# Two token groups for expert 0, more expert weights loaded ahead, and a dispatch that turns tokens by block transposes

## The chip, the cores and the metric

The kernel runs on one core of a Trainium2 chip. The metric is the device time of one execution in microseconds, the median of several. Engines are named as in the profile: PE is TensorE, PEld its loads of weights, DVE is VectorE, ACT is ScalarE, POOL is GpSimd and SP is SyncE, from which the weights' transfers are issued.

## The reference, cut to what matters

Two layers of an encoder on 256 tokens of width 1024. Each layer mixes (convolution and attention), then feeds forward: the first layer with a dense SwiGLU, the second with eight experts of which each token takes two. The change is in this last part:

```python
def moe_swiglu(h, w_router, b_router, w_gate, w_up, w_down):
    t = h.reshape(B * S, D)                                   # 256 x 1024
    logits = (t @ w_router).astype(jnp.float32) + b_router.astype(jnp.float32)
    top_val, top_idx = lax.top_k(logits, TOP_K)               # 2 of 8
    top_w = jax.nn.softmax(top_val, axis=-1)
    combine = jnp.sum(jax.nn.one_hot(top_idx, N_EXPERTS, dtype=jnp.float32)
                      * top_w[..., None], axis=1).astype(t.dtype)
    out = jnp.zeros_like(t)
    for e in range(N_EXPERTS):
        out = out + combine[:, e:e + 1] * swiglu(t, w_gate[e], w_up[e], w_down[e])
    return out.reshape(B, S, D)
```

Each expert has weights of 1024 x 3584 for gate, the same for up, and 3584 x 1024 for down, in float32: 42 MiB an expert, 336 MiB in all. Here `t` is the modulated, normalised residual `x`. With the reference's inputs expert 0 gets 34 tokens and the others 99, 66, 75, 39, 78, 58 and 63.

## The kernel before, in words

**Trunk.** The first layer and the mixing of the second come first and take some 520 us. The expert part follows.

**Slots.** The experts are worked on in eight slots. Slot 0 is always expert 0; slots 1 to 7 are the other experts, sorted by their number of tokens, which the kernel finds out as it runs. A slot has room for `CAPS[e]` groups of 32 tokens. A slot with four groups (slot 1) is *wide*: its matmuls run in three passes on weights split in two parts, hi (`half_hi`, on ACT, L147) and lo (`half_lo`, on DVE, L155), of 1 MiB of weights each. All other slots are *narrow*: the tokens are the stationary operand, 32 columns at a time, four column groups of the array work side by side, and the weights move as they were loaded (`streams`, L1096). If a slot's room isn't enough, a loop behind the kernel (`rest`) redoes the expert part for what was left over; it is not entered with these inputs.

**Units.** A slot's work is cut into seven units. One unit is gu, the gate and up products for 512 hidden columns (4 MiB of weights), and dn, the down product for them (2 MiB). In the program the dn of a unit stands behind the gu of the unit after it. Two lanes of slots (`LANES`) run by turns, lane 1 beginning after three units of lane 0 (`STAGGER`). Between gu and dn of a narrow unit stand silu and product (`sg`, `mh`), and `h_T`, which turns the hidden values by 16 block transposes on DVE (hT, L1141). Where a wide unit follows, these transposes are put off into the middle of it.

**Dispatch.** Ahead of a slot's first unit, `dispatch` brings its tokens into the slot's order: `slot_pick` makes a selection matrix `pm`; `gather` multiplies `x_sb` (the tokens, as stationary operand) with `pm` as moving operand, two halves of 16 matmuls (L1036), so that the result has the model's width on the partitions; ACT scales and shifts it by the modulation (xf, L1040); DVE copies it into the slot's `xn` (L1060). Behind it come small matmuls (`ps_ws`) for the gates and `pmT`, from which `combine` later returns the results to the tokens' order. The dispatch of a lane's next slot stands behind gu of the last but one unit of the slot before, so that it falls between two units of the other lane.

**Loads.** The weights come in half chunks of 1 MiB, all issued from SP in the order of use, each into a buffer of some pool (`raw`, `hi`, `lo`, or the working tiles `a8` of 1 MiB and `a4` of half a MiB). A load waits for whoever used its buffer last. `need(k)` issues all loads up to chunk k; `mk` in it chooses the pool by the half chunk's number `m`. `EARLY` says how many chunks are asked for before the expert part's schedule begins; the first 16 half chunks, by `SPARE8` and `SPARE4`, can lie in tiles that the trunk uses elsewhere.

**Order.** In the expert part the program's order is the engines' order (`tc.manual_schedule`); each engine works in order and waits where an operand isn't ready.

Of the kernel before, what the change touches and what calls it, by code (L numbers as in the profile page):

```python
# [9 lines left out]
F32 = mybir.dt.float32  # L10
# [20 lines left out]
PT1 = (29, 49, 15, 36)  # L31
RAW = 9
AUX = 29
SPARE8 = (0, 10, 11)
SPARE4 = (1, 6, 8)
EARLY = 7
CAPS = (3, 4, 3, 3, 3, 2, 2, 2)
LANES = (0, 1, 2, 3), (5, 6, 4, 7)
STAGGER = 3
HOME = (0, None, 0, None, 768, 768, 1536, 1536)  # L40
NR = NE - 1
EPS = 1e-6
NORM = D ** 0.5 / -8192.0
# [11 lines left out]
def kernel(ctx, tc, x, cvec, wada, bada, wga, wqkv, wout, wfgu, wfd, wfd2,  # L55
# [12 lines left out]
    def bank(name):  # L68
        return pb.tile([P, 512], F32, tag="b", name=name)
# [59 lines left out]
    def load(ap, n=4096, mk=lambda s: (rawp, "raw", G)):  # L129

        raw = []
        for h in range(n // G):
            src = ap[h] if isinstance(ap, list) else ap[:, h * G:h * G + G]
            pool, tag, w = mk(h)
            raw.append([])
            for o_ in range(0, G, w):
                r = pool.tile([P, w], F32, tag=tag, name="raw", bufs=bufs.get(tag))
                nc.sync.dma_start(r, src[:, o_:o_ + w])
                raw[-1].append(r)
        return raw  # L140
# [61 lines left out]
    def need(k):  # L202
        while len(raws) <= min(k, len(plan) - 1):
            i = len(raws)
            ap, n = plan[i]

            def mk(h):
                m = 2 * (i - first_gu) + h
                if m in SPARE8:
                    return pools["wk"], "a8", G  # L210
                if m in SPARE4:
                    return pools["wk"], "a4", G // 2
                if i < first_gu + 6:
                    return rawp, "raw", G
                turn[0] += 1
                if any(n_ for _, n_ in plan[i - 6:i + 3]):
                    return (rawp, "raw", G) if turn[0] % 10 else (pools["wk"], "a8", G)
                at = turn[0] % 16
                return ((rawp, "raw", G), (hip, "hi", G), (lop, "lo", G), (pools["wk"], "a8", G))[
                    (at >= 9) + (at >= 12) + (at >= 15)]  # L220

            raws.append(load(ap() if callable(ap) else ap, n or 4096, mk))

    def ahead(nhi, nlo=None, pre=True):
# [20 lines left out]
    def whole(lead=1):  # L245

        k = [i for i, (_, n) in enumerate(plan) if n == 0][wholes[0]]
        wholes[0] += 1
        need(k + lead)

        def rows(h, i):

            r = raws[k][h]
            n = 4 // len(r)
            return r[i // n][:, i % n * 512:i % n * 512 + 512]
        return rows
# [661 lines left out]
    def moe(acc, g_bc, mm, A, B, AW, bw):  # L918
# [109 lines left out]
        def gather(pm, n, put):  # L1028

            for q in range(2):  # L1030
                ps = bank("ps_g").rearrange("p (j s) -> p j s", j=4)
                f = a2("xf", [P, 4, P])
                for j in range(4):
                    k = 4 * q + j
                    for t in range(NT):
                        nc.tensor.matmul(ps[:, j, 0:n], x_sb[:, t, k * P:(k + 1) * P], pm[:, 1, t, 0:n],  # L1036
                                         start=t == 0, stop=t == NT - 1)
                for j in range(4):
                    k = 4 * q + j
                    nc.scalar.activation(f[:, j, 0:n], ps[:, j, 0:n], AF.Identity, scale=A[:, k:k + 1],  # L1040
                                         bias=B[:, k:k + 1])
                put(slice(4 * q, 4 * q + 4), f[:, :, 0:n])

        def dispatch(e, pm):


# [12 lines left out]
                def put(js, f):  # L1059
                    nc.vector.tensor_copy(xg[:, js, :], f)  # L1060

            gather(pm, n, put)
            ps = bank("ps_ws")
            ws = sm.tile([P, 4], F32, tag="ws", name="ws")

# [470 lines left out]
```

## Time and profile before

| | |
|---|---|
| median of 3 runs | 1374.87 us (1374.77 to 1375.17) |
| the profiled execution, its own time | 1380.11 us |
| its span, first to last instruction | 1378.4 us |
| mean granted clock of PE | 0.988 |
| PE busy | 1316.5 us (96%) |
| DVE busy | 773.1 us (56%) |
| ACT busy | 371.4 us (27%) |
| moved by DMA | 473.64 MB, mean 344 GB/s |

All times in views are microseconds from the start of the span. The profiled execution is 5.2 us longer than the median of the timed ones; what is worked out from its rows has to be set against its own time. Busy shares are over the whole span, and the expert part (from 523.7 us) has stages with different limits, so they are read by stage. PE counts as busy from the start of a matmul to its modelled end, and matmuls of the four column groups overlap, so that a PE shown as busy can still wait for little things.

### The profile page before, as it was taken

The numbers are of one execution on the slowest core, as the hardware profiler recorded it, in microseconds if no ns is written. First come the engines' busy times: TensorE is split into PE (matmuls) and PEld (weight loads), VectorE is DVE, ScalarE is ACT, GpSimd is POOL, SyncE is SP. The second block draws the span as 40 slices with busy tenths as digits, with TensorE's granted clock in tenths as the row PEclk, the third lists the DMA queues.
The fourth block names the chain that finished last, engine by engine and source line by source line (L and its number), as shares of the span: only waits on it lengthen the run. The fifth ranks groups of instructions, "written<-read, shape, count | busy, mean of one in ns | idle before, by whom it ended". The sixth has DMA issues, their size and how long they took to land.

```text
span 1378.4 us, 38871 instructions
## 1 busy us (share of the span) xinstructions
PE 1316.5 (96%) x17220; PEld 971.7 (70%) x17220; DVE 773.1 (56%) x1832; ACT 371.4 (27%) x574; POOL 3.1 (0%) x18
## 2 busy tenths in 40 slices
PE   4998989999989899999999999999999999999996
PEld 4877689999788676666667667766766776666663
DVE  3498677777679955234476666753343343334253
ACT  3335344444364522101244345401000000100000
POOL 0000000000000000000000000000000000000000
PEclk9999999999999999999999999999999999999998
DMA  9972687888561549999989999999999999999994
GB/s 384 400 291 82 256 298 282 305 300 299 196 235 41 183 154 372 402 420 425 363 354 427 398 419 407 399 411 425 423 425 423 425 424 424 400 420 417 424 425 188
DMA packets 66383, 473.64 MB, mean 344 GB/s; under 512 B 7840, under 2 KB 7968, under 8 KB 9248
## 3 DMA queue, kind: packets, MB, share of 16 engines
q1 hardware_dynamic: 66208, 471.09, 84.7%
q8 instruction: 137, 2.24, 0.6%
q14 instruction: 38, 0.31, 0.1%
HBM read 470.01 MB, written 1.05 MB: 342 GB/s over the span
## 4 chain that ended last, share of the span: by engine, by line
PE 81%; DMA 8%; DVE 6%; ACT 3%; issue 1%; SPq 0%; ACTq 0%; DVEq 0%
PE ps_gu L1096 26%; PE ps_d L1096 13%; DMA raw<-in_wmd 4%; PE ps_ga L267 4%; PE ps_ga L265 4%; PE ps_ga L266 4%; DMA raw<-in_wmgu 3%; PE ps_g L1036 2%; PE ps_y L719 2%; PE ps_gu L267 2%; PE ps_gu L265 2%; PE ps_gu L266 2%; DVE cv L555 2%; PE ps_ada L319 2%; DVE lo L155 1%; PE ps_f L265 1%
## 5 line engine op out<-in xcount | busy, mean ns | idle before, releaser
L1096 PE MATMUL ps_gu<-raw,xn 128*32 128x256 f32 x8064 | 445.8, 379 | 1.3 <-DMA raw<-in_wmgu 0.7
L1096 PEld LDWEIGHTS ps_gu<-raw,xn 128*32 128x32 f32 x8064 | 279.7, 110 | 155.9 <-issue 2.4
L155 DVE TENSOR_TENSOR lo<-raw,hi 128x2048 fp32r<-128x2048 f32 x99 | 225.8, 2290 | 79.5 <-ACT hi L147 79.0
L1096 PE MATMUL ps_d<-raw,hT 128*32 128x256 f32 x4032 | 228.4, 379 | 2.6 <-DMA raw<-in_wmd 2.4
L1130 DVE TENSOR_TENSOR mh<-ps_gu,sg 128x256 f32<-128x256 f32 (+1 forms) x91 | 32.5, 382 | 343.0 <-ACT sg L1127 342.8
L147 ACT ACTIVATE hi<-raw 128x2048 fp32r<-128x2048 f32 x99 | 188.3, 1913 | 113.2 <-PE ps_ga L267 43.0
L1141 DVE STREAM_TRANSPOSE hT<-mh 32x96 f32<-32x96 f32 (+1 forms) x784 | 200.2, 255 | 13.5 <-PE ps_bc L384 0.2
L1096 PEld LDWEIGHTS ps_d<-raw,hT 128*32 128x32 f32 x4032 | 136.2, 110 | 85.1 <-DMA raw<-in_wmd 4.0
L1127 ACT ACTIVATE sg<-ps_gu 128x256 f32<-128x256 f32 (+1 forms) x91 | 31.9, 351 | 567.1 <-PE ps_gu L1096 521.8
L265 PE MATMUL ps_ga<-hThi,lo 128*128 128x256 f32 x480 | 137.9, 287 | 7.5 <-ACT hThi L457 7.5
L267 PE MATMUL ps_ga<-hTlo,hi 128*128 128x256 f32 x480 | 137.1, 286 | 0.5 <-DVE hTlo L462 0.5
L266 PE MATMUL ps_ga<-hThi,hi 128*128 128x256 f32 x480 | 136.6, 285 | 0.0
L265 PEld LDWEIGHTS ps_ga<-hThi,lo 128*128 128x128 f32 x480 | 93.2, 194 | 8.6 <-ACT hThi L457 8.4
L267 PEld LDWEIGHTS ps_ga<-hTlo,hi 128*128 128x128 f32 x480 | 92.5, 193 | 1.2 <-DVE hTlo L462 1.2
L266 PEld LDWEIGHTS ps_ga<-hThi,hi 128*128 128x128 f32 x480 | 92.8, 193 | 0.2
L555 DVE SCALAR_TENSOR_TENSOR cv<-zp,cols_sb,cv 128x256 f32<-128x256 f32 x206 | 85.4, 476 | 0.0
L358 DVE SCALAR_TENSOR_TENSOR ada_acc<-raw,cs,ada_acc 128x512 f32<-128x512 f32 x63 | 47.2, 749 | 1.2
L267 PE MATMUL ps_gu<-lo,xg 128*128 128x512 f32 x112 | 44.5, 397 | 1.6 <-DVE lo L155 1.6
L265 PE MATMUL ps_gu<-hi,xg 128*128 128x512 f32 x112 | 44.5, 397 | 0.0
L266 PE MATMUL ps_gu<-hi,xg 128*128 128x512 f32 x112 | 44.1, 394 | 0.0
L319 PE MATMUL ps_ada<-raw,crep 128*32 128x128 f32 x960 | 34.3, 302 | 7.6 <-DMA raw<-in_wada 7.2
L319 PEld LDWEIGHTS ps_ada<-raw,crep 128*32 128x32 f32 x960 | 29.1, 121 | 11.4 <-issue 8.6
(265 smaller groups left out, 1269.1 us busy)
## 6 DMA issues: line engine op xcount, KB each, us to landing
raw<-in_wmgu SPq DMA_DIRECT2D x222, 1024.0 KB, 15.0
raw<-in_wmd SPq DMA_DIRECT2D x111, 1024.0 KB, 15.7
raw<-in_wada SPq DMA_DIRECT2D x48, 1024.0 KB, 6.3
raw<-in_wfgu SPq DMA_DIRECT2D x22, 1024.0 KB, 5.9
raw<-in_wqkv SPq DMA_DIRECT2D x12, 1024.0 KB, 6.9
raw<-in_wfd SPq DMA_DIRECT2D x11, 1024.0 KB, 6.8
raw<-in_wga SPq DMA_DIRECT2D x8, 1024.0 KB, 11.1
raw<-in_wout SPq DMA_DIRECT2D x8, 1024.0 KB, 7.0
```

Source lines behind the costliest of these rows:

```text
L147: nc.scalar.activation(hi[:, i * w:(i + 1) * w], r, AF.Copy)
L155: nc.vector.tensor_tensor(lo[:, w], r, hi[:, w].bitcast(F32), op=ALU.subtract)
L265: nc.tensor.matmul(o_, a[1], b[0], start=first, stop=False)
L266: nc.tensor.matmul(o_, a[0], b[0], start=False, stop=False)
L267: nc.tensor.matmul(o_, a[0], b[1], start=False, stop=last)
L319: nc.tensor.matmul(ps[32 * g:32 * g + 32, 0:P], crep[:, j, :], w(j)[:, g * P:(g + 1) * P], start=j == 0, stop=j == KT - 1)
L358: nc.vector.scalar_tensor_tensor(accs[ch], ws[ch](j), cs[:, j:j + 1], accs[ch], op0=ALU.mult, op1=ALU.add)
L555: nc.vector.scalar_tensor_tensor(cv[:, a, :], zp[:, a, i:i + S], cw[:, a, i:i + 1], cv[:, a, :], op0=ALU.mult, op1=ALU.add)
L1096: nc.tensor.matmul(ps[t // 2][32 * j:32 * j + 32, t % 2], x(t), w(j), start=first and t % 2 == 0, stop=last, skip_group_check=True)
L1127: nc.scalar.activation(sg[:, 2 * b:2 * b + m, :], v[:, 0:m, 0, :], AF.Silu)
L1130: nc.vector.tensor_tensor(hm[:, 2 * b:2 * b + m, :], v[:, 0:m, 1, :], sg[:, 2 * b:2 * b + m, :], op=ALU.mult)
L1141: nc.vector.transpose(hT[32 * q:32 * q + 32, :, j], v[32 * j:32 * j + 32, :, q])
```

## The change

Four things change. (1) `CAPS[0]` goes from three groups to two, and lane 1 runs slots 4, 5, 6, 7 where it ran 5, 6, 4, 7; `HOME` (where a slot's `xn` lies) follows. (2) Instead of 16 half chunks, 20 have a buffer of their own ahead of the expert part: the string `FIRST` names a pool for each ("8" and "4" are `a8` and `a4`, r, h, l are `raw`, `hi`, `lo`), `RING` for those behind where no wide unit is near, and `EARLY` is 9. (3) The last chunk, the down weights of the last unit, is loaded in eight pieces of 256 KB, by rows in the order of use. (4) Narrow slots other than slot 0 are dispatched by `spread` in place of `gather`: `pm` is the stationary operand, 32 columns of it, and `x_sb` moves, 256 columns at a time, in four column groups. The result has the tokens on the partitions; for each half ACT copies it to SBUF (`tk`), 16 block transposes on DVE turn it (xf), and ACT scales and shifts it into `xn`.

```diff
-SPARE8 = (0, 10, 11)
-SPARE4 = (1, 6, 8)
-EARLY = 7
-CAPS = (3, 4, 3, 3, 3, 2, 2, 2)
-LANES = (0, 1, 2, 3), (5, 6, 4, 7)
+FIRST = "84rrrr4rhlrhlhl488rr"
+RING = "rrrrrhlrhlhlr8rr"
+EARLY = 9
+CAPS = (2, 4, 3, 3, 3, 2, 2, 2)
+LANES = (0, 1, 2, 3), (4, 5, 6, 7)
...
             def mk(h):
                 m = 2 * (i - first_gu) + h
-                if m in SPARE8:
-                    return pools["wk"], "a8", G
-                if m in SPARE4:
-                    return pools["wk"], "a4", G // 2
...
+                if m < len(FIRST):
+                    at = FIRST[m]
...
+            if i == len(plan) - 1:
+
+                raws.append([])
+                for j, src in enumerate(zip(*[v.rearrange("p (k n) -> k p n", k=4) for v in ap()])):
+                    r = rawp.tile([P, 2, 512], F32, tag="raw", name="raw")
+                    for h in range(2):
+                        nc.sync.dma_start(r[:, h, :], src[h])
+                    raws[-1].append(r)
+                continue
...
+        def spread(pm, g, xg):
+
+
+            pv = [bank(f"ps_g{b}").rearrange("p (t s) -> p t s", t=2) for b in range((g + 1) // 2)]
+            for t in range(g):
+                for tt in range(NT):
+                    for j in range(4):
+                        nc.tensor.matmul(pv[t // 2][32 * j:32 * j + 32, t % 2], pm[:, 1, tt, 32 * t:32 * t + 32],
+                                         x_sb[:, tt, 256 * j:256 * j + 256], start=tt == 0 and t % 2 == 0,
+                                         stop=tt == NT - 1, skip_group_check=True)
+            for h in range(2):
+                tk = a2("tk", [P, g, P])
+                for b, v in enumerate(pv):
+                    m = min(2, g - 2 * b)
+                    nc.scalar.activation(tk[:, 2 * b:2 * b + m, :], v[:, 0:m, h * P:h * P + P], AF.Copy)
+                v = tk.rearrange("p t (q s) -> p t q s", q=4)
+                f = a2("xf", [P, 4, 32 * g])
+                for j in range(4):
+                    for q in range(4):
+                        nc.vector.transpose(f[32 * q:32 * q + 32, j].rearrange("p (t s) -> p t s", s=32),
+                                            v[32 * j:32 * j + 32, :, q])
+                    k = 2 * j + h
+                    nc.scalar.activation(xg[:, k, :], f[:, j, :], AF.Identity, scale=A[:, k:k + 1], bias=B[:, k:k + 1])
...
-            gather(pm, n, put)
+            if e and not wide(e):
+                spread(pm, g, xg)
+            else:
+                gather(pm, n, put)
```

DVE in the middle of a wide unit's gu, where lane 1's second slot is dispatched (lo is the second part of 1 MiB of the wide unit's weights, mh the hidden values of the other lane's unit), before:

```order
L155 TENSOR_TENSOR lo_7493<-raw_7381,hi_7489 128x2048
L155 TENSOR_TENSOR lo_7495<-raw_7383,hi_7491 128x2048
L1060 COPY xn_4926<-xf_7498 128x256
L1060 COPY xn_4926<-xf_7513 128x256
L1084 TENSOR_SCALAR pmT_7547<-ps_ws_7527,spot_96 128x256 x2
L1085 COPY ws_7528<-ps_ws_7527 128x2
L155 TENSOR_TENSOR lo_7559<-raw_7417,hi_7557 128x2048
L155 TENSOR_TENSOR lo_7575<-raw_7419,hi_7573 128x2048
L1141 STREAM_TRANSPOSE hT_7613<-mh_7462 32x2x32 x16
```

and now:

```order
L155 TENSOR_TENSOR lo_7453<-raw_7307,hi_7449 128x2048
L155 TENSOR_TENSOR lo_7455<-raw_7309,hi_7451 128x2048
L1073 STREAM_TRANSPOSE xf_7476<-tk_7474 32x64 x16
L1073 STREAM_TRANSPOSE xf_7499<-tk_7497 32x64 x16
L1121 TENSOR_SCALAR pmT_7540<-ps_ws_7520,spot_96 128x256 x2
L1122 COPY ws_7521<-ps_ws_7520 128x2
L155 TENSOR_TENSOR lo_7552<-raw_7359,hi_7550 128x2048
L155 TENSOR_TENSOR lo_7568<-raw_7361,hi_7566 128x2048
L1178 STREAM_TRANSPOSE hT_7606<-mh_7420 32x3x32 x16
```

Two copies stood between the second and the third lo; two sets of 16 transposes stand there now, and the other lane's hT has three groups instead of two.

ACT at the same place, before:

```order
L147 ACTIVATE hi_7489<-raw_7381 128x2048
L147 ACTIVATE hi_7491<-raw_7383 128x2048
L1040 ACTIVATE xf_7498<-ps_g_7497,vcol_106,A2_1_4638 128x64 x4
L1040 ACTIVATE xf_7513<-ps_g_7512,vcol_106,A2_1_4638 128x64 x4
L147 ACTIVATE hi_7557<-raw_7417 128x2048
L147 ACTIVATE hi_7573<-raw_7419 128x2048
```

and now:

```order
L147 ACTIVATE hi_7449<-raw_7307 128x2048
L147 ACTIVATE hi_7451<-raw_7309 128x2048
L1068 ACTIVATE tk_7474<-ps_g0_7457 128x256
L1076 ACTIVATE xn_4926<-xf_7476,vcol_106,A2_1_4638 128x64 x4
L1068 ACTIVATE tk_7497<-ps_g0_7457 128x256
L1076 ACTIVATE xn_4926<-xf_7499,vcol_106,A2_1_4638 128x64 x4
L147 ACTIVATE hi_7550<-raw_7359 128x2048
L147 ACTIVATE hi_7566<-raw_7361 128x2048
```

The writes of xn, which wait for DVE's transposes, now stand ahead of the wide unit's third hi.

DVE where slot 2 is dispatched, ahead of the last dn of the wide slot (hTlo is that dn's stationary operand), before:

```order
L1148 TENSOR_TENSOR hTlo_8504<-ps_hT_8498,hThi_8503 128x512
L1060 COPY xn_4926<-xf_8508 128x384
L1060 COPY xn_4926<-xf_8523 128x384
L1084 TENSOR_SCALAR pmT_8565<-ps_ws_8537,spot_96 128x256 x3
L1085 COPY ws_8538<-ps_ws_8537 128x3
L155 TENSOR_TENSOR lo_8647<-raw_8462,hi_8643 128x2048
L155 TENSOR_TENSOR lo_8649<-raw_8464,hi_8645 128x2048
```

and now:

```order
L1185 TENSOR_TENSOR hTlo_8581<-ps_hT_8575,hThi_8580 128x512
L1073 STREAM_TRANSPOSE xf_8613<-tk_8610 32x96 x16
L1073 STREAM_TRANSPOSE xf_8637<-tk_8634 32x96 x16
L1121 TENSOR_SCALAR pmT_8686<-ps_ws_8658,spot_96 128x256 x3
L1122 COPY ws_8659<-ps_ws_8658 128x3
L155 TENSOR_TENSOR lo_8768<-raw_8539,hi_8764 128x2048
L155 TENSOR_TENSOR lo_8770<-raw_8541,hi_8766 128x2048
```

Here too the transposes of the dispatch now stand ahead of both lo's of the dn.

## Rows read from the trace of the kernel before

**Rows 1.** The page's part 4: shares of the chain that ended last, by engine.
```profile
PE 81%; DMA 8%; DVE 6%; ACT 3%; issue 1%; SPq 0%; ACTq 0%; DVEq 0%
```
**Rows 2.** That chain in order of time: start us, us, what.
```profile
731.90 7.04 PE ps_gu L1096 x128
...
919.74 8.72 DMA raw<-in_wmgu
928.58 21.01 DMA raw<-in_wmd
...
1342.97 19.45 DMA raw<-in_wmd
1362.47 3.67 PE ps_d L1096 x60
```
**Rows 3.** Waits of SP's queue, 440 to 560 us: total us, times, longest.
```profile
SPq L138 <- PE ps_gu L1096: 21.9, 3, 15.6
```
**Rows 4.** Windows: PE, PEld, DVE, ACT, POOL busy us (count), PEclk, DMA share, GB/s.
```profile
700.00:720.00 20.00, 20.00 (x232) 13.63 (x225) 12.63 (x9) 11.09 (x8) 0.00 (x0) 1.00 0.80 309
...
880.00:900.00 20.00, 20.00 (x234) 13.04 (x232) 13.44 (x34) 4.97 (x5) 0.00 (x0) 1.00 1.01 426
...
1180.00:1200.00 20.00, 20.00 (x361) 14.59 (x355) 6.28 (x23) 3.24 (x10) 0.00 (x0) 1.00 0.99 394
```
**Rows 5.** Groups by shape: busy us, mean ns of one, idle before by releaser.
```profile
L147 ACT ACTIVATE hi<-raw 128x2048 fp32r<-128x2048 f32 x99 | 188.3, 1913 | 113.2 <-PE ps_ga L267 43.0 <-issue 32.5 <-PE ps_d L266 12.7
L1141 DVE STREAM_TRANSPOSE hT<-mh 32x96 f32<-32x96 f32 x448 | 120.9, 270 | 7.9 <-PE ps_bc L384 0.2
...
L1127 ACT ACTIVATE sg<-ps_gu 128x256 f32<-128x256 f32 x63 | 24.1, 383 | 565.5 <-PE ps_gu L1096 521.8 <-PE ps_gu L267 43.7
...
L1040 ACT ACTIVATE xf<-ps_g,vcol,A 128x64 f32<-128x64 f32 x24 | 7.7, 403 | 17.9 <-PE ps_g L1036 17.9
```
**Rows 6.** PE's timeline at lane 1's dispatch in the wide unit: start, us, what.
```profile
744.58 3.68 PE L1036 MATMUL ps_g<-pm,x_sb 128*128 128x64 f32 x32
...
749.05 0.51 PE L265 MATMUL ps_gu<-hi,xg 128*128 128x512 f32 x1
...
760.45 1.92 PE L1096 MATMUL ps_d<-raw,hT 128*32 128x256 f32 x30
```
**Rows 7.** DVE's timeline there.
```profile
751.43 2.29 DVE L155 TENSOR_TENSOR lo<-raw,hi 128x2048 fp32r<-128x2048 f32 x1 [0.66 <-ACT hi L147]
...
756.09 4.03 DVE L1141 STREAM_TRANSPOSE hT<-mh 32x64 f32<-32x64 f32 x16
```
**Rows 8.** PE's timeline at slot 2's dispatch.
```profile
854.42 3.71 PE L1036 MATMUL ps_g<-pm,x_sb 128*128 128x96 f32 x32
...
859.00 7.11 PE L1096 MATMUL ps_gu<-raw,xn 128*32 128x256 f32 x128
866.04 0.50 PE L265 MATMUL ps_d<-hi,hTlo 128*128 128x512 f32 x1
```
**Rows 9.** DVE's timeline there.
```profile
861.40 4.50 DVE L155 TENSOR_TENSOR lo<-raw,hi 128x2048 fp32r<-128x2048 f32 x2 [0.20 <-ACT hi L147]
```
**Rows 10.** PE's timeline in a combine, with the idle time ahead of it.
```profile
802.45 0.50 PE L1206 MATMUL ps_sc<-yhi,pmT 32*128 32x256 f32 x3 [1.34 <-DVE mh L1130]
```
**Rows 11.** Windows behind that stop, columns as in rows 4.
```profile
804.70:808.20 3.50, 3.50 (x10) 2.72 (x9) 2.37 (x2) 0.43 (x1) 0.00 (x0) 0.51 1.01 428
808.20:812.00 3.80, 3.80 (x18) 3.02 (x18) 2.29 (x1) 2.69 (x2) 0.00 (x0) 1.00 1.02 427
```
**Rows 12.** DMA issues at 916.2 to 916.6 us: count, KB each, us to landing.
```profile
raw<-in_wmgu SPq DMA_DIRECT2D x1, 1024.0 KB, 7.2
```
**Rows 13.** DMA issues at 447 to 452 us, the same columns.
```profile
raw<-in_wmgu SPq DMA_DIRECT2D x1, 1024.0 KB, 5.0
```
**Rows 14.** PE's timeline at the end: the dn before the last.
```profile
1357.52 3.69 PE L1096 MATMUL ps_d<-raw,hT 128*32 128x256 f32 x64 [1.19 <-DMA raw<-in_wmd]
```

More of the change, by code (lines that the diff above doesn't have):

```diff
@@ L33 @@
 AUX = 29
-SPARE8 = (0, 10, 11)
-SPARE4 = (1, 6, 8)
-EARLY = 7
-CAPS = (3, 4, 3, 3, 3, 2, 2, 2)
-LANES = (0, 1, 2, 3), (5, 6, 4, 7)
+FIRST = "84rrrr4rhlrhlhl488rr"
[3 more added lines that the diff above has]
+LANES = (0, 1, 2, 3), (4, 5, 6, 7)
 STAGGER = 3
-HOME = (0, None, 0, None, 768, 768, 1536, 1536)
+HOME = (0, None, 0, None, 768, 1536, 768, 1536)
 NR = NE - 1
@@ L208, in mk @@
                 m = 2 * (i - first_gu) + h
-                if m in SPARE8:
-                    return pools["wk"], "a8", G
-                if m in SPARE4:
-                    return pools["wk"], "a4", G // 2
-                if i < first_gu + 6:
-                    return rawp, "raw", G
[L215 to L220, printed above, removed]
+                if m < 0:
+                    return rawp, "raw", G
+                if m < len(FIRST):
+                    at = FIRST[m]
+                elif any(n_ for _, n_ in plan[i - 6:i + 3]):
+                    turn[0] += 1
+                    at = "8" if turn[0] % 10 == 0 else "r"
+                else:
+                    at = RING[(m - len(FIRST)) % len(RING)]
+                return {"r": (rawp, "raw", G), "h": (hip, "hi", G), "l": (lop, "lo", G), "8": (pools["wk"], "a8", G),
+                        "4": (pools["wk"], "a4", G // 2)}[at]
+            if i == len(plan) - 1:
[6 more added lines that the diff above has]
+                continue
             raws.append(load(ap() if callable(ap) else ap, n or 4096, mk))
@@ L251, in rows @@
         def rows(h, i):
+            if k == len(plan) - 1:
+                return raws[k][i][:, h, :]
             r = raws[k][h]
@@ L1060, in put @@
                     nc.vector.tensor_copy(xg[:, js, :], f)
-            gather(pm, n, put)
+            if e and not wide(e):
+                spread(pm, g, xg)
+            else:
+                gather(pm, n, put)
             ps = bank("ps_ws")
```

## The prediction, made before the changed kernel ran

> **What bounds the kernel now.** I read the chain of waits first, by engine and then in order of time, then the windows, then the PE, DVE and ACT timelines around the places that the change touches. The reader should see three stages. Up to 919.7 us of the span the chain runs on PE: the page gives PE 81% and DMA 8% [rows 1], and no transfer stands in the expert part before the one at 919.74 [rows 2]. So up to there a microsecond more or less on PE is a microsecond on the end, if the loads follow. In this stage loads wait for PE to free buffers: SP waited 21.9 us for the first expert matmuls, 15.6 of it for one buffer [rows 3], and the engines of the DMA are at 0.80 and 309 GB/s in 700 to 720 us, while PE is busy for all of its 20 us [rows 4]. From 880 us the transfers run at 1.01 and 426 GB/s [rows 4]. From 919.74 the chain is a chain of transfers: the load issued then took 8.72 us to land, the next one in the chain 21.01, and the last one, issued at 1342.97, took 19.45 and released the final PE piece at 1362.47 [rows 2]. After 919.74 work on PE is hidden behind transfers; what counts is how late the loads are by then, and what comes behind the last of them.
>
> **The first groups, one lane exchanged, more chunks ahead.** Slot 0 gives up a group of three, and slot 4 with three groups takes the early place that slot 5 with two had. With 7 units of each, up to the end of the wide stage as much PE work is removed as added: each narrow unit is 192 matmuls with three groups and 128 with two, and 128 take 7.04 us [rows 2], 55 ns each, so a group is 64 of them or 3.5 us in either place. I cost this at 0. The combines of the two slots exchange a group in the same way. The first dispatch still gathers; its eight writes of 403 ns [rows 5] get a little shorter, which I count at nothing. The inputs of the reference send 34 tokens to expert 0, so that two groups of 32 hold them, and the path for overflow isn't taken.
>
> The earlier loads remove waits of SP like the one of 15.6 us [rows 3], and the stream is then ahead by most of that at its start. I cost it at 0: PE is the bound, so a chunk that lies ready earlier is not used earlier, and by 700 us the queue is idle a fifth of the time anyway [rows 4]. The lead cannot outgrow the buffers, whose number doesn't change.
>
> **The new dispatch on PE.** A gather with two groups is 32 matmuls in 3.68 us [rows 6], with three groups 3.71 [rows 8]. spread has 8 matmuls for each group, of the shape of the expert matmuls (32 columns of weights, 256 columns moving, four column groups at a time). At 55 ns three groups take 24 x 0.055 = 1.3 us and two take 0.9. With 0.2 us for filling the array that is a gain of 2.2 us with three groups and of 2.6 with two. Were the four not to overlap, each would take its own 379 ns or so, 24 x 0.38 = 9.1 us, a loss of 5.4 us; I take the first price, since the shape is one that this kernel runs so thousands of times. For slot 4, dispatched in the narrow part of the PE stage, this is **-2.2 us**. Those of slots 6, 3 and 7 lie behind 919.74, where transfers hide PE: 0.
>
> **The new dispatch on DVE and ACT, slot 5.** This is where I see the cost. The order of the changed kernel puts the 32 transposes ahead of the two lo's with which the wide unit goes on, and on ACT the tk's and the scaled writes ahead of the hi's from which those lo's are made. Call the start of the dispatch on PE T0; before it was 744.58, the wide matmuls began at 749.05, the first lo behind the dispatch ran from 751.43 to 753.72, and the other lane's matmuls followed at 760.45, which is T0 + 15.9 [rows 6, 7]. Now: matmuls to T0 + 1.3 (0.9 and an end like the others' 0.4), a tk like the sg of 383 ns [rows 5] to T0 + 1.7, sixteen transposes, which took 4.03 us for hT [rows 7], to T0 + 5.7, and a last scaled write of 0.4 [rows 5] to T0 + 6.1. The second half's tk stands behind these writes on ACT: T0 + 6.5, transposes to T0 + 10.5, write to T0 + 10.9. Then hi, 1.91 us [rows 5], to T0 + 12.8, lo, 2.29, to T0 + 15.1, and the second lo to T0 + 17.4. PE, with its gather shorter by 2.6, wants the first of these lo's 5.6 us (half of its 11.2) behind the start of the wide matmuls, that is at T0 + 4.5 - 2.6 + 5.6 = T0 + 7.5. It stands for some 7 us. Its second half, 5.6 us from T0 + 15.1, ends at T0 + 20.7; the hT transposes, sixteen of 270 ns [rows 5] since slot 4 has three groups, come behind the second lo and end at T0 + 21.9. The other lane's matmuls begin between these two, against T0 + 15.9 before: +4.8 to +6.0, and I take **+5.6**, since before they began 0.3 us behind the transposes [rows 6, 7].
>
> **The same for slot 2.** T0 was 854.42, the narrow unit's matmuls ran from 859.00 for 7.11 us, and the wide dn began at 866.04, T0 + 11.6; its two lo's ran from 861.40 to 865.90, so hardly ahead of it [rows 8, 9]. Now with 270 ns a transpose: two tk's to T0 + 2.3, transposes to T0 + 6.6, write to T0 + 7.0, tk's to T0 + 7.7, transposes to T0 + 12.0, write to T0 + 12.4, hi to T0 + 14.3, lo to T0 + 16.6. The dn's third matmul needs it half a microsecond in: the dn is late by 16.6 - 0.5 - 11.6 = 4.5, and with a little overlap I take **+4.3**.
>
> **The clock.** At 802.45 PE had stood for 1.34 us; in 804.7 to 808.2 the granted clock was 0.51, the level of 1.2 GHz, and 10 matmuls took 3.50 us, where 18 took 3.80 at 1.00 right behind [rows 10, 11]. That is 10 x (0.350 - 0.211) = 1.4 us lost. I expect one such stretch behind each of the two stops of 5 to 7 us: **+2.8** (ends 0 and, twice as long, +5.6).
>
> **From PE to the loads.** PE is then late by -2.2 + 5.6 + 4.3 + 2.8 = 10.5 us at 916. A load issued at 916 landed 7.2 us later, against 5.0 for one that found the queue empty [rows 12, 13]: 2.2 us of queue drain first, **-2.2**. In 1180 to 1200, at a dispatch, the rate fell to 394 of 426 GB/s [rows 4], 20 x 0.075 = 1.5 us; the shorter dispatch on PE may give half of that back, **-0.7** (ends 0 and -1.5).
>
> **The last chunk in pieces.** Before, the last dn waited for both whole MiB: the dn before it ended at 1357.52 + 3.69 = 1361.2, the last began at 1362.47 [rows 2, 14]. In pieces of 256 KB in the order of use it can begin as the one before ends: **-1.3**. The last piece still lands when it did, and a quarter of the dn has to follow it; the ends are 0 and -2.5 (the dn's 3.67 but for its last quarter). Nothing smaller than 1 MiB is loaded there before, so the price of pieces isn't in the trace. The Trainium skill (DMA: Bandwidth & Descriptors, Measured) advises transfers of at least 1 MiB for three quarters of the peak; by that estimate the last 2 MiB, 4.9 us at 426 GB/s, would take some 1.6 us longer and the sum be higher by 2.9. No row of before shows it.
>
> **Sum.** 10.5 - 2.2 - 0.7 - 1.3 = +6.3. The profiled execution took 1380.11 us (span 1378.4), 5.2 over the median of 1374.87; a profiled run of the changed kernel would be at 1386.4, and the median at **1381.2**.
>
> **Rivals.** First, the transposes are hidden: what speaks for it is that DVE is busy for 12.63 of 20 us in 700 to 720 [rows 4]; against it that DVE works in order and the lo's stand behind. Then PE gains 2.2 + 2.6 before the transfers are full, and what slot 2 gains finds a full queue [rows 4]: -4.8 - 0.7 - 1.3 = -6.8, **1368**. Second, the stops are half as long, because hi's or transposes run earlier than I think, and the clock holds: -2.2 + 5.0 - 2.2 - 0.7 - 1.3 = -1.4, **1373.5**, not to be told from before; the hi's, which need no transposed data, speak for it, their place on ACT against. Third, transfers and not PE decide from the start, so that the lead of the early loads (15.6 less a landing or so, 11 to 13 us) reaches the end: **1361**; the DMA share of 0.80 [rows 4] speaks against. Fourth, it is worse: the lateness carries without the queue's 2.2, the low clock lasts twice as long, or the pieces come slowly: +9 to +13, **1384 to 1388**.
>
> **How the numbers follow.** Forecast 0.47, hidden 0.17, half 0.22, early loads 0.04, worse 0.10. About 0.2%, 2.7 us, can be told from no change, so up to 1377.6 counts as the same, and under 1372.1 as faster. Faster is 0.17 + 0.04 and a little of the second rival, 0.22; the same is the rest of the second and the near edge of the forecast, 0.23; slower 0.55. The forecast's own range is 1376 to 1385. From 1367 to 1387 no more than 2 in 10 is left out: the early loads, part of the first rival and the end of the worst.
>
> **What would show it.** Right: in the timeline of PE two stops of 4 to 7 us before matmuls of the wide unit, released by DVE's lo, each with transposes from tk on DVE in that time and a granted clock near 0.5 behind; DMA share below 1 there; a chain that turns to transfers around 930; a last dn that starts as the one before ends. Wrong: no such stops, or loads that wait for nobody ahead of 919 us; spread matmuls at more than 100 ns each; a transposing sixteen far from 4 to 4.6 us.

## The result: slower, by about twice what was forecast

| | median us | lowest to highest, runs | ratio of the runs to those of before |
|---|---|---|---|
| before | 1375.44 | 1373.76 to 1383.55, 11 | |
| changed | 1386.56 | 1385.48 to 1397.39, 11 | 1.0096, 95% interval 1.0074 to 1.0118 |

The medians differ by 11.1 us; the ratio makes it 13.2 (10.2 to 16.2). Forecast were +6.3 us and 1381.2. The time lies in the range given, at its upper edge, and the sign was right; the forecast size was about half of what came. Executions of one kernel lay up to 12 us apart, the longer ones with a lower mean granted clock (here 0.980 at 1385.5 us and 0.974 at 1397.4), so differences of two or three microseconds are read from the traces below.

The profiled execution of the changed kernel took 1385.48 us, span 1383.8. Against the span of before that is only +5.4. But in the trace of before the gather of slot 0 begins at 516.6 us and in this one at 512.5: 4.1 us that lie in the trunk. The earlier half chunks need have no part in that: over all traces of this study this gather begins between 512.3 and 516.5 us with them and between 510.8 and 516.6 without. So the rest of this document counts from the dispatch of slot 0, where the difference is +9.5 us. The traces thus account for 9.5 of the 11.1 us between the medians; what the rest consists of is not traced.

The chain of the profile's page, then its pieces in order of time (start, us, what), which answer to [rows 1, 2]. The page follows this chain back to 873 us only, so the shares are small:

```profile
DMA 30%; PE 6%; DVE 0%; issue 0%; SPq 0%; ACT 0%; ACTq 0%
```
```profile
873.44 2.30 DVE lo L155
...
927.99 3.48 PE ps_gu L1133 x64
931.47 10.97 DMA raw<-in_wmd
```

It reads as forecast: a lo on DVE, PE behind it, and from 931.47 on transfers, but for four pieces of PE of some 5 us each ahead of the last dn. What PE waited for between 700 and 920 us (us in total, times, longest), first in the kernel before, then in the changed one:

```profile
PE ps_sc L1206 <- DVE mh L1130: 1.3, 1, 1.3
```
```profile
PE ps_gu L275 <- ACT hi L147: 4.9, 1, 4.9
PE ps_d L275 <- ACT hi L147: 4.7, 1, 4.7
PE ps_sc L1243 <- DVE mh L1167: 1.5, 1, 1.5
PE ps_gu L277 <- DVE lo L155: 1.1, 1, 1.1
PE ps_d L277 <- DVE lo L155: 1.1, 1, 1.1
```

Four waits of 11.8 us in all are new: both stops are there, each in two steps, first for hi, then for lo. PE's and DVE's timeline at the first (start, us, what, idle time ahead and releaser; they answer to [rows 6, 7]):

```profile
733.62 1.93 PE L1061 MATMUL ps_g<-x_sb,pm 128*32 128x256 f32 x32
...
747.21 0.79 PE L275 MATMUL ps_gu<-hi,xg 128*128 128x512 f32 x1 [4.85 <-ACT hi L147]
749.54 0.79 PE L277 MATMUL ps_gu<-lo,xg 128*128 128x512 f32 x1 [1.11 <-DVE lo L155]
757.31 5.39 PE L1133 MATMUL ps_d<-raw,hT 128*32 128x256 f32 x96
```
```profile
736.04 4.03 DVE L1073 STREAM_TRANSPOSE xf<-tk 32x64 f32<-32x64 f32 x16 [1.10 <-ACT tk L1068]
740.85 4.03 DVE L1073 STREAM_TRANSPOSE xf<-tk 32x64 f32<-32x64 f32 x16 [0.78 <-ACT tk L1068]
...
747.19 4.50 DVE L155 TENSOR_TENSOR lo<-raw,hi 128x2048 fp32r<-128x2048 f32 x2 [1.33 <-ACT hi L147]
```

PE stands until 747.2 and again until 749.5, while DVE transposes; the other lane's matmuls follow at 757.31. The second stop, on DVE and then on PE, and windows of both stops (columns as in [rows 4]):

```profile
861.00 4.57 DVE L1073 STREAM_TRANSPOSE xf<-tk 32x96 f32<-32x96 f32 x16 [1.75 <-ACT tk L1068]
866.54 4.57 DVE L1073 STREAM_TRANSPOSE xf<-tk 32x96 f32<-32x96 f32 x16 [0.97 <-ACT tk L1068]
...
873.44 4.49 DVE L155 TENSOR_TENSOR lo<-raw,hi 128x2048 fp32r<-128x2048 f32 x2 [0.96 <-ACT hi L147]
```
```profile
873.46 0.80 PE L275 MATMUL ps_d<-hi,hTlo 128*128 128x512 f32 x1 [4.69 <-ACT hi L147]
...
875.79 0.80 PE L277 MATMUL ps_d<-lo,hThi 128*128 128x512 f32 x1 [1.10 <-DVE lo L155]
```
```profile
749.50:757.30 7.80, 7.76 (x22) 5.88 (x22) 6.83 (x18) 0.00 (x0) 0.00 (x0) 0.65 0.74 271
757.30:765.00 7.70, 7.70 (x137) 4.54 (x140) 1.11 (x2) 2.00 (x3) 0.00 (x0) 1.00 0.14 36
875.80:881.30 5.50, 5.50 (x13) 4.39 (x14) 4.67 (x3) 2.75 (x2) 0.00 (x0) 0.51 0.95 349
```

Behind each stop the clock is low: 0.65 as a mean of 7.8 us behind the first, 0.51 over 5.5 us behind the second. And the DMA engines run dry behind the first: 0.14 and 36 GB/s, since SP had to wait for buffers that lo and PE's dn free, 14.0 us for the first (SP's waits in 735 to 775 us: in total, times, longest):

```profile
SPq L138 <- DVE lo L155: 17.6, 3, 14.0
SPq L138 <- PE ps_d L1133: 10.5, 1, 10.5
```

### The profile page after: what moved, and what is told of

It is laid out like the page before. It is cut to its first block, busy times and chain, and to the rows that moved or that the text cites. A ratio compares the mean times of both kernels' runs of the same rounds, so it can differ in the third digit from the quotient of the medians.

```text
span 1383.8 us, 37778 instructions
## 1 busy us (share of the span) xinstructions
PE 1283.1 (93%) x16564; PEld 926.2 (67%) x16564; DVE 811.0 (59%) x2003; ACT 379.3 (27%) x585; POOL 3.1 (0%) x18
## 5 line engine op out<-in xcount | busy, mean ns | idle before, releaser
L1133 PE MATMUL ps_gu<-raw,xn 128*32 128x256 f32 x7616 | 432.1, 379 | 21.1 <-DMA raw<-in_wmgu 21.1
L1133 PEld LDWEIGHTS ps_gu<-raw,xn 128*32 128x32 f32 x7616 | 259.3, 110 | 179.8 <-DMA raw<-in_wmgu 31.7
L1133 PE MATMUL ps_d<-raw,hT 128*32 128x256 f32 x3808 | 223.4, 380 | 10.1 <-DMA raw<-in_wmd 10.1
L1178 DVE STREAM_TRANSPOSE hT<-mh 32x64 f32<-32x64 f32 (+1 forms) x784 | 196.4, 251 | 13.6 <-PE ps_bc L394 0.2
L1133 PEld LDWEIGHTS ps_d<-raw,hT 128*32 128x32 f32 x3808 | 129.8, 110 | 91.5 <-DMA raw<-in_wmd 15.0
L1073 DVE STREAM_TRANSPOSE xf<-tk 32x96 f32<-32x96 f32 (+1 forms) x192 | 48.6, 253 | 19.9 <-ACT tk L1068 16.8
L275 PE MATMUL ps_gu<-hi,xg 128*128 128x512 f32 x112 | 46.5, 415 | 4.9 <-ACT hi L147 4.9
L276 PE MATMUL ps_gu<-hi,xg 128*128 128x512 f32 x112 | 46.0, 410 | 0.0
## 6 DMA issues: line engine op xcount, KB each, us to landing
raw<-in_wmd SPq DMA_DIRECT2D x109, 1024.0 KB, 19.4
raw<-in_wga SPq DMA_DIRECT2D x8, 1024.0 KB, 10.8
```

The lines of the kernel that those rows point to most:

```text
L275: nc.tensor.matmul(o_, a[1], b[0], start=first, stop=False)
L276: nc.tensor.matmul(o_, a[0], b[0], start=False, stop=False)
L1073: nc.vector.transpose(f[32 * q:32 * q + 32, j].rearrange("p (t s) -> p t s", s=32), v[32 * j:32 * j + 32, :, q])
L1133: nc.tensor.matmul(ps[t // 2][32 * j:32 * j + 32, t % 2], x(t), w(j), start=first and t % 2 == 0, stop=last, skip_group_check=True)
L1178: nc.vector.transpose(hT[32 * q:32 * q + 32, :, j], v[32 * j:32 * j + 32, :, q])
```

## The experiments

Each run has its ratio to the kernel before in the same series; the median of the kernel before was 1375.5 to 1375.8 in all of them.

| run | what differs | median us | ratio to before, 95% interval |
|---|---|---|---|
| e1 | changed, gather for slots 5 and 2 | 1377.41 | 1.0013, 0.9989 to 1.0038 |
| e2 | changed, gather everywhere | 1381.51 | 1.0016, 0.9989 to 1.0043 |
| e9 | changed, gather for slot 5 | 1390.24 | 1.0102, 1.0079 to 1.0125 |
| e8 | changed, lo's ahead of the transposes | 1389.16 | 1.0102, 1.0059 to 1.0144 |
| e10 | e2 without the additional early loads | 1375.05 | 0.9998, 0.9974 to 1.0023 |
| e3 | e2 with the lanes of before | 1346.92 | 0.9782, 0.9747 to 0.9816 |
| e4 | changed, lanes of before | 1368.52 | 0.9935, 0.9909 to 0.9961 |
| e5 | before, two groups in slot 0 | 1357.71 | 0.9862, 0.9826 to 0.9899 |
| e6 | e3, spread for slots 5 and 7 | 1344.87 | 0.9771, 0.9738 to 0.9805 |
| e7 | e3, spread for 5, 4, 3, 7, tk's first | 1344.83 | 0.9785, 0.9750 to 0.9821 |
| e11 | e7 with the last chunk whole | 1347.12 | 0.9796, 0.9772 to 0.9820 |

### Without the transposes among wide units (e1, e2, e9)

```diff
-            if e and not wide(e):
+            if e and not wide(e) and e not in (5, 2):
                 spread(pm, g, xg)
```

> The changed kernel with gather instead of spread for the two dispatches that fall among wide units (slots 5 and 2); the others spread. Theory (the transposes ahead of the lo's stop PE twice, and this lateness reaches the end): the idle times of 4.85 + 1.11 and 4.69 + 1.10 us before L275 to L277 go, with the low clock behind them; 7.8 + 8.4 = 16 us less on PE by 920 us, of which the loads give back some 3 less, so 1386.3 - 13 = 1373, within 2 us. Rival (the exchanged lane, the earlier loads or the pieces of the last chunk cost the time): the stops go, but the time stays above 1383.

Measured: 1377.41, of twelve runs the lowest 1373.17, against 1386.56 and 1385.48 in the changed kernel. The difference is 9 us between the medians and 12 between the lowest, where the theory has 13 within 2; the median lies 2.4 above its band. The trace settles it, because the dispatch of slot 5 happens to begin at the same microsecond in both. PE with gather there, and what PE waited for in 700 to 920 us:

```profile
733.62 3.68 PE L1046 MATMUL ps_g<-pm,x_sb 128*128 128x64 f32 x32
...
749.48 2.80 PE L1133 MATMUL ps_d<-raw,hT 128*32 128x256 f32 x48
```
```profile
PE ps_sc L1243 <- DVE mh L1167: 1.5, 1, 1.5
```

From the same 733.62 the other lane's matmuls come at 749.48 instead of 757.31: 7.8 us for the first stop, its clock included and spread's shorter matmuls already taken off. All four waits are gone. The last transfer lands 12.2 us earlier (1357.4 against 1369.6). The rival, that the time stays without the stops, fell: the two stops together make the difference between the changed kernel and the kernel before.

In the second run gather stands everywhere.

> The changed kernel with gather in every dispatch: all parts of the change but spread. Theory: as with gather at the two places, about 1373 to 1374, since slot 4's dispatch gains only 0.8 us by spread (2.80 us of matmuls instead of 3.71) and slots 6, 3 and 7 are dispatched while PE has time. Rival (spread is worth its 1 to 2 us at each of four places): 3 to 6 us above the kernel that gathers at two places only.

1381.51, with five of twelve runs from 1372.2 to 1375.4 and seven from 1381.4 up; its ratio, 1.0016, is that of e1, 1.0013. So spread at slots 4, 6, 3 and 7 moves nothing that can be measured here. The medians alone, 4 us apart, would have said otherwise; the intervals say the two are not told apart.

With gather at slot 5 alone:

> The changed kernel with gather for slot 5 only; slot 2 is still dispatched by spread among wide units. Theory (the two stops are alike and add up): the first stop of 4.85 + 1.11 us goes, the second stays, and the time lies about halfway between the changed kernel (1386.3) and gather at both places (1374 to 1377): 1380 to 1382. Rival (loads that stand after one stop absorb the second, or the first): at one of the two ends, under 1378 or over 1385.

1390.24, 1382.95 to 1392.39: not the halfway that was expected, a miss. By its median the time came out at the end that the rival names (over 1385), so the timed runs don't show that the two stops add up. In the trace of the fastest of these runs PE gains the 7.8 us at the first stop: the dispatch begins 2.9 us later than in the changed kernel, the dn behind it 4.95 earlier. But 3.0 of these 4.95 are lost again at the next combine, where the clock is low in 800 to 810 us behind a wait of 1.47 us:

```profile
800.00:810.00 10.00, 8.54 (x47) 6.91 (x43) 6.50 (x7) 1.72 (x2) 0.00 (x0) 0.66 1.01 419
```

In the changed kernel the same wait, 1.46 us, was followed by a clock of 1.00. In e9's trace the last transfer lands 2.6 us earlier than in the changed kernel's. Why the median shows nothing of that is open; six runs that lie 9 us apart can't tell. Gather at slot 2 alone was not run, so what each stop costs by itself is known from the traces only.

### Is it only the order? (e8)

```diff
-                    ahead(2)
+                    ahead(3 if nxt == 5 else 2)
...
+                    if wide(pend[0]) and not wide(nxt):
+                        ahead(2)
+                        ready.append(1)
                     disp[nxt] = dispatch(nxt, pm)
```

> The changed kernel with one more hi and lo of the wide unit ahead of slot 5's dispatch, and both of the dn's ahead of slot 2's. Rival (only the order is at fault): both stops go, and the time falls to that of gather at these places, 1374 to 1377. Theory (DVE has too much to do in that stretch: between the dispatch of slot 5 and the other lane's matmuls 2 lo's of 2.29, two sets of transposes of 4.03 and hT of 4.57 are 17 us against 14 us of PE work): the stop moves to the last lo and hT but is 4 to 6 us long still at slot 5, and halved at slot 2: 1378 to 1383.

1389.16: no better than the changed kernel. The lo's do run first, and then something else is late. At slot 2, DVE, then PE:

```profile
864.45 4.57 DVE L1073 STREAM_TRANSPOSE xf<-tk 32x96 f32<-32x96 f32 x16
873.86 4.57 DVE L1073 STREAM_TRANSPOSE xf<-tk 32x96 f32<-32x96 f32 x16 [4.85 <-issue]
```
```profile
881.05 0.79 PE L275 MATMUL ps_gu<-hi,xg 128*128 128x512 f32 x1 [6.82 <-ACT hi L147]
```

The dn now has its operands, but the hi's and lo's of the next gu come behind the transposes, and PE stands there for 6.82 us, longer than the 4.69 that were removed. The first stop is 3.67 + 1.11 us instead of 4.85 + 1.11. So this order doesn't help: at slot 5 most of the stop stays, as the theory has it, since the DVE and ACT work of the dispatch doesn't fit between the weights' conversions. At slot 2 that isn't shown: behind the stop of 6.82 us lies a gap of 4.85 on DVE for which the profile names no releaser. The second half's tk was there at 869.95. The gap ends at 873.86, just behind the last matmul of the wide dn that reads hTlo (873.38 and 0.39 us), and hTlo and xf come from the same pool of buffers (`a2`); a wait for that buffer would fit, but no run shows it. The estimate of 1378 to 1383 had not seen the wait coming back one step later.

### What the exchanged lane costs (e3, e4, e5)

```diff
-LANES = (0, 1, 2, 3), (4, 5, 6, 7)
+LANES = (0, 1, 2, 3), (5, 6, 4, 7)
-HOME = (0, None, 0, None, 768, 1536, 768, 1536)
+HOME = (0, None, 0, None, 768, 768, 1536, 1536)
```

> As with gather everywhere, and lane 1 in the order of before (5, 6, 4, 7): slot 0 has two groups, and slot 4's three groups are not brought forward. Theory (up to 920 us PE is the bound, and the exchanged lane gives back the 36 us that slot 0's third group saved there): PE is ahead by up to 36 us at 920, the loads become the bound much earlier, the early half chunks count, and the time falls to 1350 to 1360. Rival (transfers set the time, whatever PE does there): no better than 1370.

1346.92, 28.9 us under before and 34.6 under the same kernel with lane 1 as changed (e2). The part of the change that I had costed at 0, because as much work is added as removed, gives away some 36 us of PE work at the place where it counts most: in 700 to 800 us the transfers run at 360 GB/s in e2 and at 417 in e3. With the lanes of before slot 4 is dispatched behind the wide stage, and its third group runs later. The chain was expected to turn to transfers much earlier; it did so at 575.66 us, for four loads, and did not stay there. From 650 us PE is on the chain to the end:

```profile
PE 83%; DMA 6%; DVE 6%; ACT 3%; issue 1%; SPq 0%; DVEq 0%; ACTq 0%
```

So the time fell further than expected, by 3 us, and for another reason than a bound by transfers. These are hardly less full, though: 414 to 425 GB/s in every stretch from 520 to 1284 us. With spread in that order:

> The changed kernel with spread as it is, but lane 1 in the order 5, 6, 4, 7. Theory: the two stops of PE among wide units stay (5 to 6 us each in the timeline, released by lo), but PE has the 36 us of slot 0's third group in hand, so that they cost little of the end: within 4 us of the same lanes with gather, far under before. Rival (each stop also stops the loads and is lost for good): 8 to 13 us above the same lanes with gather.

1368.52, 21.6 us above e3. The theory (PE has 36 us in hand, so stops cost little) fell clearly, and the rival's 8 to 13 is too small too. In e3 PE has nothing in hand, it is the bound, and so the stops are paid; and there are four, of 19.4 us in all. PE's waits in 700 to 1080 us:

```profile
PE ps_gu L1133 <- ACT tk L1068: 7.3, 2, 3.7
PE ps_gu L275 <- ACT hi L147: 4.9, 1, 4.9
PE ps_d L275 <- ACT hi L147: 4.7, 1, 4.7
PE ps_gu L277 <- DVE lo L155: 1.4, 1, 1.4
...
PE ps_d L277 <- DVE lo L155: 1.1, 1, 1.1
```

The two of 3.7 us are a kind that I had not thought of. They stand behind the dispatches of slots 4 and 3, in narrow matmuls: gu with three groups needs two PSUM banks, and the second is held by spread's result until the second tk has been copied; that tk stands behind four scaled writes, each of which waits for transposes (PE, then ACT's copies of the second tk):

```profile
946.62 11.39 PE L1133 MATMUL ps_gu<-raw,xn 128*32 128x256 f32 x176 [3.67 <-ACT tk L1068]
```
```profile
946.21 0.53 ACT L1068 ACTIVATE tk<-ps_g 128x256 f32<-128x256 f32 x2
```

The changed kernel has no such wait that matters: slot 4 is dispatched elsewhere, and behind 920 us its PE waits for transfers anyway, 25.5 us up to 1340.

Of the kernel before, the group alone:

```diff
-CAPS = (3, 4, 3, 3, 3, 2, 2, 2)
+CAPS = (2, 4, 3, 3, 3, 2, 2, 2)
```

> The kernel before with one number changed: slot 0 has two groups instead of three (its loads, lanes, gather and last chunk stay). Theory (PE sets the time, so the 36 us of PE work that this group was are most of the gain, and the early half chunks give what is left): 1352 to 1357, that is 5 to 10 us above the 1346.9 of the old lanes with gather and the early loads. Rival (the early half chunks are what lets the freed time count): above 1362.

1357.71: 18 us gained by one number, 10.8 less than e3, which differs by the early loads and by the pieces of the last chunk (for these see e11). The theory had 5 to 10. What the early half chunks are worth in this order shows in 590 to 660 us, where PE waits for transfers, first without them, then with them (e3):

```profile
PE ps_gu L1096 <- DMA raw<-in_wmgu: 7.2, 6, 1.7
PE ps_d L1096 <- DMA raw<-in_wmd: 4.5, 4, 1.7
```
```profile
PE ps_gu L1133 <- DMA raw<-in_wmgu: 2.6, 2, 1.4
PE ps_d L1133 <- DMA raw<-in_wmd: 1.7, 1, 1.7
```

11.7 us against 4.3. PE's work after that is 8 us later without them, up to the last dn, which then waits 2.7 us for its chunk.

### The early loads in the changed order (e10)

```diff
-FIRST = "84rrrr4rhlrhlhl488rr"
+FIRST = "84rrrr4r4r88"
-EARLY = 9
+EARLY = 7
```

> The changed kernel with gather everywhere and only as many half chunks loaded ahead as before (12 placed, seven chunks asked for). Theory (with slot 4 in lane 1's first place PE sets the time up to 920 us, so a lead of the loads is worth nothing): within 2 us of the same kernel with the 20 early half chunks. Rival (the lead of the loads, some 13 us at the start of the expert part, reaches the end): 6 to 13 us slower than it.

1375.05 against 1381.51 with them; ratios 0.9998 and 1.0016, each within the other's interval, so the timed runs show no loss without the early loads. In the traces PE without them is 1.5 us ahead at the dispatch of slot 0 (the trunk), level at 957 us and 1.3 behind at the last dn. Counted from that dispatch it loses 2.8 us: 1.2 in the wide gu at 660 us and the combine behind it, where of these two traces only this one has the low clock, 0.3 up to 957 us and 1.3 later. So the term of 0 holds for this order within some 3 us, and only for it.

### Where spread pays, and the pieces of the last chunk (e6, e7, e11)

```diff
-            if e and not wide(e):
+            if e in (5, 7):
                 spread(pm, g, xg)
```

> Old lanes, gather except for slots 5 and 7, which are dispatched by spread: the two places where the trace of spread with the old lanes shows no stop behind the dispatch and PE 1.85 us earlier. Theory (what spread saves on PE counts in full where nobody waits for DVE or ACT): 1346.9 - 3.7 = 1343.2, within 1.5. Rival (transposes cost elsewhere what PE saves): 1346 or more.

1344.87, 2 us under e3; expected were 1343.2 within 1.5, so a little less than the theory has, and the ratio's interval does not tell it from e3. In the trace each of the two dispatches makes PE 1.85 us earlier, as expected. But what slot 5's gives is gone by 650 us, in waits for transfers (6.5 us in 590 to 660 us against 4.3 in e3), and behind slot 7's 1.2 us are spent on a wait for a transfer at the end.

```diff
-            for h in range(2):
-                tk = a2("tk", [P, g, P])
+            tks = [a2("tk", [P, g, P]) for h in range(2)]
+            for h in range(2):
...
-                    nc.scalar.activation(tk[:, 2 * b:2 * b + m, :], v[:, 0:m, h * P:h * P + P], AF.Copy)
+                    nc.scalar.activation(tks[h][:, 2 * b:2 * b + m, :], v[:, 0:m, h * P:h * P + P], AF.Copy)
```

> Old lanes; spread for slots 5, 4, 3 and 7 with both tk's ahead of the scaled writes on ACT, gather for slots 6 and 2 (among wide units). Theory (the stops of 3.67 us behind the dispatches of slots 4 and 3 come from the PSUM bank that the second half's tk frees late, behind four writes that wait for DVE): those stops go, and PE is 0.9 us earlier there as well: 1341.5, within 2. Rival (DVE's 32 transposes themselves hold PE up there): stops of over 1 us remain in the timeline behind these dispatches and the time is above 1346.

1344.83: the stops are gone, as the theory of the PSUM bank wants, and its rival fell. Behind the dispatch of slot 4, PE in one piece:

```profile
925.90 10.57 PE L1134 MATMUL ps_gu<-raw,xn 128*32 128x256 f32 x192
```

PE gains 1.0 us at each of slots 4 and 3 besides, and is 8.3 us ahead of e3 at 1300 us in these traces (4.2 of it from the trunk). But the time stays at e6's, 1.3 us above the theory's band around 1341.5: the last stretch waits for transfers now, as the row of e7 below shows. In this order a faster dispatch gives no more. e6 and e7 are the fastest kernels of this study, 30.8 us under before.

> Old lanes, spread for slots 5, 4, 3 and 7 with both tk's first, as in the run of 1344.8, but the last chunk in two whole MiB. There the loads are the last to end. Theory (the pieces let the last dn start before its second MiB is there): 1.3 us slower, the last dn's start 1.3 us behind the one before it in PE's timeline. Rival (small transfers cost what they save): the same or faster.

1347.12, 2.3 us slower, with intervals that overlap. The traces show the mechanism. PE's last dn with whole MiB and, below it, in pieces (e7):

```profile
1323.89 3.67 PE L1134 MATMUL ps_d<-raw,hT 128*32 128x256 f32 x64 [1.20 <-DMA raw<-in_wmd]
1328.76 3.65 PE L1134 MATMUL ps_d<-raw,hT 128*32 128x256 f32 x60 [1.19 <-DMA raw<-in_wmd]
```
```profile
1322.86 7.10 PE L1134 MATMUL ps_d<-raw,hT 128*32 128x256 f32 x124 [1.20 <-DMA raw<-in_wmd]
```

Whole, the last dn waits 1.19 us for its second MiB; in pieces the two dn's are one block. (The 1.20 us ahead of both are the wait of the dn before the last.)

## Why the prediction was half right

The places, the reasons and the sign were right. What failed are two terms of the sum for PE, the new dispatch and the clock: the two stops cost 16.1 us with their low clock where 12.7 were forecast, and slot 4's dispatch gained 0.8 where 2.2 were.

**The two stops: right.** Both came at the places, for the reasons and about with the lengths forecast: the end of DVE's lo was forecast for slot 5 at T0 + 15.1 and came at T0 + 15.9; the other lane's matmuls followed at T0 + 23.7 instead of T0 + 15.9. e1 shows that the two stops together are the cause; e8 shows that the order tried there doesn't remove them.

**What bounds: too coarse.** [rows 2] leave out what stands in the chain of before between 949.63 and 1284.00, and there it is PE:

```profile
949.63 5.37 PE ps_d L1096 x92
...
1272.72 10.43 PE ps_gu L1096 x192
```

The page's DMA 8% is 110 us, a quarter of what comes behind 919.74. So in the kernel before PE was not hidden there: its trace shows no wait of PE between 920 and 1340 us, while from 950 us on the transfers ran at 417 to 424 GB/s; both were full. In the changed kernel, which has a group less to work on there, PE does wait for transfers, so what the forecast took from that reading held for it.

**PE was late by 15.8 us, not 10.5.** From the traces, counted from the dispatch of slot 0: the start of the expert part -0.7; slot 4's dispatch -0.8 (forecast -2.2); a low clock and 0.4 us more of waiting in a wide gu +2.6 and a shorter combine -1.0 (forecast none); slot 5's dispatch +7.8 (forecast 5.6 + 1.4); the next combine -0.4; slot 2's +8.3 (forecast 4.3 + 1.4). That sums to 15.8. Three steps were off; the first two make up most of the difference.

The first is *the new dispatch on PE*. I counted 24 and 16 matmuls for spread, from the program; the trace has 48 and 32, as it has 32 where gather's program has 16. A float32 matmul of the program is two in the trace, and the price of 55 ns that I used is one trace entry's:

```profile
L1061 PE MATMUL ps_g<-x_sb,pm 128*32 128x256 f32 x240 | 14.9, 380 | 0.0
```

The six spreads, three with three groups and three with two, ought to have 120 entries by my count and have 240. With three groups it takes 2.8 us where I had 1.5, gather takes 3.7; so spread saves 0.9 us on PE with three groups and 1.8 with two, and not 2.2 and 2.6. Its transposes begin later, too: the first lo behind them ends 0.8 us later than forecast at slot 5 and 1.3 at slot 2.

The second is *the clock*. I took 1.4 us for each stop from one stretch of 3.5 us. Behind the second stop 13 matmuls lie in 5.5 us [the window above], 13 x (0.423 - 0.222) = 2.6 us with 27 matmuls in 6.0 us right behind for the full clock; behind the first, the second half of gu took 7.8 us instead of 5.6, so 2.2. That is 4.8 for both where I had 2.8; the upper end of that term, 5.6, was nearer. The Trainium skill (TensorE: Matmul & The Clock Gate, HAM oscillation) says that a wait for data, if it is long enough, sets TensorE back to the low level, that this happens again at each such wait, and that work at 1.2 GHz takes twice its time. The trace agrees behind both long stops (0.65 and 0.51, and some 0.43 us from one matmul to the next where it is 0.23 at the full clock).

The third is the low clock that I had not forecast, +2.6, in the wide gu that begins at 660 us. It stands behind a wait of 1.59 us for lo that both kernels have; before, the clock did not fall behind it (first row), now it did (second row):

```profile
684.00:700.00 16.00, 14.41 (x105) 11.28 (x107) 13.62 (x28) 5.10 (x5) 0.00 (x0) 1.00 0.99 409
```
```profile
660.00:680.00 20.00, 17.91 (x122) 13.08 (x122) 16.89 (x29) 5.53 (x6) 0.00 (x0) 0.91 0.97 408
```

The change only moved this stretch. In 10 of the 13 traces of this study the clock is low in the 7 us behind this wait, and the kernel before is one of the three where it isn't. That is a chance; [rows 11] had the price of such a stretch, but not where one would come. It weighs little in the end: behind the next combine it is the other way round, the low clock of [rows 11] is gone (-1.5), and a group more costs 1.1 there, which makes the -0.4.

**From PE to the loads: forecast -2.9, found -4.5.** PE is late by 15.8 and the last transfer by 7.2 + 4.1 = 11.3. Whether it was the queue's drain, the dispatch of slot 6 or something else that gave back more was not measured.

**The last chunk: right.** PE's end is late by 5.5 + 4.1 = 9.6 where the last transfer is late by 11.3: 1.7 gained, forecast 1.3, and e11 shows the 1.2 us of the wait. The estimate from the rule of the Trainium skill (DMA: Bandwidth & Descriptors, Measured), 1.6 us longer, does not show: the last 2 MiB landed within 5.1 us of the load ahead of them, before within 4.9, though eight transfers of 256 KB carried them:

```profile
raw<-in_wmd SPq DMA_DIRECT2D x8, 256.0 KB, 11.4
```

**The sum of these.** -0.7 - 0.8 + 1.6 + 7.8 - 0.4 + 8.3 - 4.5 - 1.7 = +9.6, against +9.5 between the spans.

**The lane exchange at 0: right as a sum, and the costliest sentence in it.** Work removed and work added were equal, as costed, and e3 shows that they need not have been: it is the place of the added work that matters, and I had read from [rows 2] that PE sets the time up to 919.74 and is hidden behind transfers later. From that reading it follows that a group moved out of the first part is worth its whole PE work; a rival for this wasn't among mine, because I weighed the change as a whole and not its parts against each other. The price of a group was wrong as well, without an effect on the sum: 3.5 us are its gu alone, and dn adds 32 matmuls of 55 ns, so a unit has 5.3 and seven units have some 37 us.

**The rivals.** *Hidden transposes*: not so, by the waits above. *Early loads*: not seen here (e10), but with the pieces of the last chunk 10.8 us in the other order (e5 against e3), 7.4 of them in PE's waits for the loads. *Half stops*: no. *Worse*, 1384 to 1388 with a chance of 0.10: that is where it came out, with the clock low for nearly twice as long, as it said, but not for its other reasons.

## What to carry to other kernels

Before work is exchanged between two places, ask at each what sets the time there: equal work moved from a stretch where the transfers are full anyway into one that PE bounds can cost nearly its whole length, here some 30 us of time with one lane's order. A dispatch that is cheaper on one engine can be paid on the others: list what is queued behind its instructions on each in-order engine, and also which PSUM banks it holds until they are done. A chain shown in part hides what stands between: set its shares against the stretch that is left. And count matmuls in the trace's entries, not in the program's calls, when a price per entry is used.

## What the hardware showed that was not expected

A stop of TensorE of about 1.5 us is sometimes followed by the low clock and sometimes not, for the same instructions: behind 1.46 us at the same combine the mean granted clock of the next stretch was 1.00 in the changed kernel (first row) and 0.70 with gather at two slots (second row).

```profile
810.00:820.00 10.00, 10.00 (x45) 8.04 (x44) 7.65 (x4) 5.82 (x4) 0.00 (x0) 1.00 1.01 426
```
```profile
800.00:810.00 10.00, 10.00 (x44) 8.09 (x41) 5.15 (x5) 2.62 (x2) 0.00 (x0) 0.70 1.01 425
```

In the 10 us behind this combine's wait of 1.33 to 1.47 us the clock is low in 11 of the 13 traces (means of 0.66 to 0.83), and in the 7 us behind the wide gu's wait of 1.59 to 1.61 us in 10 (0.76). Such a stretch cost 1.5 us in the kernel before and 3.0 in e9, so a change that only shifts such a wait in time can move the end by that much, up or down. The nine stops of 3.67 to 6.82 us in these traces were all followed by it.
